# Differential heads stored unscaled with their norm applied once per row tile, and index query stacks filled from SBUF to SBUF, in a hybrid attention layer

## The chip, the cores and the metric

The kernel runs on one core of one Trainium2 chip. The metric is the device time in microseconds (us) of one execution; several executions are timed and their median is given. The core has five engines that matter here: TensorE (PE: matmuls and transposes), VectorE (DVE), ScalarE (ACT), GpSimd (POOL) and SyncE (SP, which issues nearly all transfers). Each engine takes its instructions from a queue of its own, strictly in order; an instruction that waits holds up all that stand behind it on the same engine.

## The reference

One transformer layer for 1024 rows of width 1024. An input projection feeds three token mixers whose outputs are concatenated (256 + 512 + 256 columns), projected, added to the input and normalised; a SwiGLU feed-forward block with a second norm follows. Two of the mixers matter here.

```python
# differential attention: 4 heads, two softmaxes each
logits = einsum('bthmd,bshmd->bhmts', qblk, k) * scale - slope * dist      # masked by chunk
p = softmax(logits)
attn = p[:, :, 0] - lam * p[:, :, 1]
o = einsum('bhts,bshe->bthe', attn, v)                                     # 128 columns per head
o = rms_norm(o, subln_g) * (1.0 - lam_init)     # o * rsqrt(mean(o*o) + 1e-5) * g, per row and head

# sparse attention: an indexer with 8 heads of width 32 picks 256 keys per row
idx_logits = einsum('bthd,bsd->bths', qi, ki)
score = einsum('bth,bths->bts', wi * idx_scale, relu(idx_logits))          # masked by chunk
_, sel = top_k(score, 256)
```

## The kernel before, in words

Rows are cut into 8 tiles of 128. Float32 products are made exact enough by splitting each operand into a rounded part and a rest (names ending in h and l) and running three matmuls per product: `mm3` (L179 to L182) issues all three. An engine's instruction order is not written out: the kernel is traced in program order, a list scheduler with a cost model orders each engine's queue, and memory and buffers are given out by the same framework, which makes an instruction wait where it reuses memory that something else still reads. Program order and `high_priority` blocks set the priorities.

The stages, by the time at which they run in the profiled execution:

- To 48 us: x is loaded, transposed and split; `proj_ik` and `proj_iq` (L240 to L252) project the index key `kst` and the index queries. `hq[c]`, `lq[c]` (c = 0, 1) hold the rounded and rest parts of four query heads each, 32 partitions per head.
- From 48 to 143 us: the index scores. Each of the 8 heads needs a stack `qst` of 128 partitions: rounded, rest, rounded, rest of its 32 rows. Before the change `hq[c]` and `lq[c]` are stored into a DRAM tile `qd[c]` (L294, L295) and four stacks are read back, each by one transfer whose source pattern has a leading dimension of 2 with step 0 (L298 to L300). `index` (L358 to L375) makes 48 steps (8 heads by 6 row tiles): matmuls `psi` (L365), a relu on ScalarE into `rl` (L367), and a weighted sum into the score buffer `sc_all` on VectorE (L370, L372).
- In between run steps of the generator `fill`, which makes the remaining projections in the order of `FILL_ORDER`: first the values of heads 0 and 1 ("v0", four steps of 48 matmuls `psn` each, L325 to L335), then the queries and keys of head 0 ("b0", four half projections of 24 matmuls `psp`). `INDEX_FILLS` says after how many index steps how many fill steps are traced; L713 to L717 do that and then run `FIRST_FILL` more steps.
- From 143 to 431 us: the differential heads, 32 units of a head and a row tile (`diff_unit`, L637 to L659), in the order of `UNITS`, with further fill steps and steps of a bisection for the 256th score (`bisect`, on VectorE and ScalarE) between them as `FILLS`, `STEPS_A` and `STEPS_D` say. A unit runs two softmaxes without normalising (`softmax`, L600 to L614: the sums of the exponentials are s1 and s2), forms p1 - lam * (s1/s2) * p2 (L645 to L648), transposes it on PE and multiplies it with the values into the one PSUM buffer of its kind, `pso` (`attend`). Then ScalarE squares `pso` scaled by 1/s1 and sums it (L655), `rsqrt` forms the norm factor with one VectorE and one POOL instruction (L192 to L198), VectorE multiplies it by 1/s1 (L657) and writes the scaled and weighted tile `ob` (L658), which SyncE stores into the DRAM tile `mixd[i]` (L659).
- From 431 to about 690 us: the sparse heads (`dsa_pair`), and per row tile `mix_in` (L801 to L812), which loads `mixd[t]` as `mx`, transposes it and splits it for the output projection (`out_half`); then the first norm (`finish1`).
- To 1372 us: the feed-forward block and the second norm.

Of the kernel before, what the change touches and what calls it, by code (L numbers as in the profile page):

```python
# [9 lines left out]
F32 = mybir.dt.float32  # L10
# [4 lines left out]
AF = mybir.ActivationFunctionType  # L15
OP = mybir.AluOpType
AX = mybir.AxisListType

P = 128
S = 1024  # L20
DM = 1024
NT = S // P
# [8 lines left out]
NH = 4  # L31
SLOPES = [2.0 ** (-2.0 * (h + 1)) for h in range(NH)]
# [3 lines left out]
EPS = 1e-5  # L36
# [4 lines left out]
LASTN = 6  # L41
FILL_ORDER = ["v0", "b0", "b1", "b2", "v2", "b3", "vc", "c0", "g", "c1"]
INDEX_FILLS = [(11, 1), (6, 1), (13, 1), (8, 1), (2, 1), (8, 1)]
FIRST_FILL = 1
GMLP_ORDER = ["uv", "u", "u", "u", "v", "v", "vs", "vs", "s", "s"]
UNITS = [
# [39 lines left out]
def pieces(n):  # L86
    r = []
    o = 0
    while o < n:
        w = min(512, n - o)  # L90
        if 0 < n - o - w < 256:
            w = n - o - 256
        r.append((o, max(w, 256)))
        o += w
    return r
# [3 lines left out]
def trunk(  # L99
# [5 lines left out]
    nc = tc.nc  # L105
# [6 lines left out]
    pool = ctx.enter_context(tc.tile_pool(name="pool", bufs=1))  # L112
    psum = ctx.enter_context(tc.tile_pool(name="psum", bufs=2, space=bass.MemoryType.PSUM))
    dram = ctx.enter_context(tc.tile_pool(name="dram", bufs=1, space=bass.MemoryType.DRAM))
# [9 lines left out]
    def st(name, shape=(P, 1024), dt=F32R):  # L124
        return tl("st", 12, name, shape, dt)
# [10 lines left out]
    def small(name, w=1, dt=F32, bufs=5):  # L136
        return pool.tile([P, w], dt, tag=f"s_{name}", bufs=bufs, name=name)
# [7 lines left out]
    def ps_qk(name):  # L145
        return psum.tile([P, 512], F32, tag="qk", bufs=3, name=name)

    def ps_av(name):
        return psum.tile([P, 512], F32, tag="av", bufs=1, name=name)

    def f(ap):
        return ap.bitcast(F32)

    V, A, GP = nc.vector, nc.scalar, nc.gpsimd
# [5 lines left out]
    def rawload(src, name, shape):  # L160
        raw = tl("raw", 2, f"raw_{name}", shape)
        nc.sync.dma_start(raw, src)
        return raw

    def wsplit(raw, name, shape, lo_eng, hi=None, lo=None):
        if hi is None:
            hi = tl("hi", 3, f"hi_{name}", shape, F32R)
            lo = tl("lo", 3, f"lo_{name}", shape, F32R)
        if lo_eng is GP:
            GP.tensor_scalar(hi, raw, 1.0, 1.0, op0=OP.mult, op1=OP.mult)  # L170
        else:
            A.activation(hi, raw, AF.Copy)
        sub(lo_eng, lo, raw, f(hi))
        return hi, lo

    def wload(src, name, shape, lo_eng, hi=None, lo=None):
        return wsplit(rawload(src, name, shape), name, shape, lo_eng, hi, lo)

    def mm3(ps, lh, ll, rh, rl, first, last):  # L179
        nc.tensor.matmul(ps, lh, rh, start=first, stop=False)  # L180
        nc.tensor.matmul(ps, lh, rl, start=False, stop=False)  # L181
        nc.tensor.matmul(ps, ll, rh, start=False, stop=last)  # L182

    def row_bcast(vec, n):
        return bass.AP(tensor=vec.tensor, offset=vec.offset, ap=[[0, P], [1, n]])
# [3 lines left out]
    mhalf = pool.tile([P, 8], F32, name="mhalf")  # L189
    V.memset(mhalf, -0.5)  # L190

    def rsqrt(o, var, eps, w, pre=None):  # L192
        t = small(f"rv{w}", w)
        if pre is None:
            V.tensor_scalar(t, var, eps, None, op0=OP.add)  # L195
        else:
            V.tensor_scalar(t, var, pre, eps, op0=OP.mult, op1=OP.add)
        GP.tensor_tensor(o, t, mhalf[:, 0:w], OP.pow)  # L198
# [48 lines left out]
    def proj_iq(c, half):  # L247
        w0, w = ((256, 256), (0, 512))[half]
        ps = proj_t(*iqw[c], P, half, w0, w)
        o = half * 512 + w0 - 256  # L250
        A.activation(hq[c][:, o:o + w], ps[:, w0:w0 + w], AF.Copy)
        sub(V, lq[c][:, o:o + w], ps[:, w0:w0 + w], f(hq[c][:, o:o + w]))  # L252

    iqw, hq, lq = [], [], []

    def load_iq(c):
        if c == 1:
            riq.append(rawload(win[:, :, I_Q + P:I_Q + 2 * P], "iq1", [P, KC, P]))
        iqw.append(wsplit(riq[c], f"iq{c}", [P, KC, P], V))
        hq.append(st(f"hq{c}", (P, 768)))  # L260
        lq.append(st(f"lq{c}", (P, 768)))
# [23 lines left out]
    V.tensor_copy(iw, pw[:, 0:64].rearrange("p (a b) -> p a b", a=NT))  # L285

    qst = []
    qd = [dram.tile([4, 2, 32, 768], F32, name=f"qd{c}") for c in range(2)]
    for c in range(2):
        if c == 1:  # L290
            load_iq(1)
            proj_iq(1, 0)
            proj_iq(1, 1)
        nc.sync.dma_start(qd[c][:, 0], f(hq[c]))  # L294
        nc.sync.dma_start(qd[c][:, 1], f(lq[c]))  # L295
        for j in range(4):
            q = st(f"qst{c}_{j}", (P, 768))
            rep = qd[c][j].rearrange("r p c -> (r p) c")  # L298
            rep = bass.AP(tensor=rep.tensor, offset=rep.offset, ap=[[0, 2], [768, 64], [1, 768]])
            nc.sync.dma_start(f(q), rep)  # L300
            qst.append(q)

    lamv = []
    for nm, (a, b) in enumerate(((lq1, lk1), (lq2, lk2))):
# [5 lines left out]
        r = small(f"lr{nm}", 1, bufs=1)  # L310
# [3 lines left out]
    neglam = small("neglam", 1, bufs=1)  # L314
# [3 lines left out]
    subg = pool.tile([P, P], F32, name="subg")  # L318
# [34 lines left out]
    o = 0  # L353
# [121 lines left out]
    junk, junk_a = junk2[:, 0], junk2[:, 1]  # L475
# [118 lines left out]
    def prob_tiles(i, c):  # L594
        if c * (i + 1) <= KC:
            t = pp("pt")
            return [t[:, j * P * (i + 1):(j + 1) * P * (i + 1)] for j in range(c)]
        return [pp("pt") for _ in range(c)]

    def softmax(i, m, q, kh, kl, bias, slope, p):  # L600
        n = P * (i + 1)
        nm = None
        sm = small("sm")
        for o, w in pieces(n):
            ps = ps_qk("psq")
            nc.tensor.matmul(ps[:, 0:w], q[:, i * P:(i + 1) * P], kh[:, o:o + w], start=True, stop=False)
            nc.tensor.matmul(ps[:, 0:w], q[:, i * P:(i + 1) * P], kl[:, o:o + w], start=False, stop=True)
            w = min(w, n - o)
            prev = BIG if nm is None else nm
            nm = small(f"nm{o}")  # L610
            V.tensor_tensor_reduce(out=p[:, o:o + w], in0=ps[:, 0:w], in1=bias[:, o:o + w], scale=-slope, scalar=prev,  # L611
                                   op0=OP.add, op1=OP.min, accum_out=nm)
        A.activation(p[:, 0:n], p[:, 0:n], AF.Exp, bias=nm, scale=-1.0, accum_out=sm)  # L613
        return p, sm  # L614
# [10 lines left out]
    def attend(i, a, vsl, ps):  # L625
        nk = i + 1
        for j0 in range(0, nk, 4):
# [6 lines left out]
            for j in range(jn):  # L634
                nc.tensor.matmul(ps, at[:, j * P:(j + 1) * P], vsl(j0 + j), start=(j0 + j == 0), stop=(j0 + j == nk - 1))  # L635

    def diff_unit(h, i, qs, kh, kl, vb):  # L637
        n = P * (i + 1)
        bias = dist[:, S - n:S]
        p1, p2 = prob_tiles(i, 2)  # L640
        _, s1 = softmax(i, 0, qs[0], kh[0], kl[0], bias, SLOPES[h], p1)
        _, s2 = softmax(i, 1, qs[1], kh[1], kl[1], bias, SLOPES[h], p2)
        r1, r2 = small("r1"), small("r2")
        sn = small("sn", 1, bufs=3)
        GP.tensor_tensor(sn, s1, neglam, OP.mult)  # L645
        V.reciprocal(r2, s2)
        V.tensor_tensor(r2, r2, sn, OP.mult)
        V.scalar_tensor_tensor(p1[:, 0:n], p2[:, 0:n], r2, p1[:, 0:n], op0=OP.mult, op1=OP.add)  # L648
        V.reciprocal(r1, s1)
        ps = ps_av("pso")  # L650
        attend(i, p1, lambda j: vb[:, j], ps[:, 0:P])
        ss = small("ss")
        ob = tl("o", 4, "ob", (P, P))
        rs = small("rs")
        A.activation(junk_a[:, 0:P], ps[:, 0:P], AF.Square, scale=r1, accum_out=ss)  # L655
        rsqrt(rs, ss, EPS, 1, pre=1.0 / P)
        V.tensor_tensor(rs, rs, r1, OP.mult)  # L657
        V.scalar_tensor_tensor(ob, ps[:, 0:P], rs, subg, op0=OP.mult, op1=OP.mult)  # L658
        nc.sync.dma_start(mixd[i][:, 256 + h * P:256 + (h + 1) * P], ob)  # L659

    bits = {e: list(range(31, -1, -1)) for e in "ad"}

# [6 lines left out]
    def run(gen, n=100):  # L669
        for _ in range(n):  # L670
            if next(gen, 0) == 0:
                break
# [22 lines left out]
    ix = index(range(8))  # L695
# [11 lines left out]
    fill = stream([g_ for k_ in FILL_ORDER for g_ in units[k_]])  # L707

    def ensure(qk, v, u):
        while min(made.get(qk + "q", 0), made.get(qk + "k", 0)) < 1 + u // 4 or made.get(v, 0) < 1 + u // 2:  # L710
            next(fill)

    for q, r_ in INDEX_FILLS:  # L713
        run(ix, q)
        run(fill, r_)
    run(ix)
    run(fill, FIRST_FILL)  # L717
    nstep = {"a": STEPS_A, "d": STEPS_D}

    def scale_rows(o, r, e):  # L720
# [80 lines left out]
    def mix_in(t):  # L801
        mx = tl("raw", 2, "mx")
        nc.sync.dma_start(mx, mixd[t])
        nh, nl, shp = f"mTh{t}", f"mTl{t}", (P, KC, P)
        if t in (3, 4):
            ms[t] = pp(nh, shp, F32R), pp(nl, shp, F32R)
        else:
            ms[t] = tl("hi", 3, nh, shp, F32R), tl("lo", 3, nl, shp, F32R)
        transpose_split(mx, *ms[t], 0, n=6)
        v = mx[:, 6 * P:].rearrange("p (a b) -> p a b", a=2)  # L810
        A.activation(ms[t][0][:, 6:8], v, AF.Copy)
        sub(GP, ms[t][1][:, 6:8], v, f(ms[t][0][:, 6:8]))  # L812
# [240 lines left out]
    for hh in range(2):  # L1053
# [8 lines left out]
        for t in range(4):  # L1062
# [4 lines left out]
            for d in range(2):  # L1067
                ps = acc[2 * t + d]
# [38 lines left out]
```

## Time and profile before

| | |
|---|---|
| median of 3 runs | 1370.33 us (1369.95 to 1374.3) |
| the profiled execution's own time | 1374.44 us |
| its span from first to last instruction | 1372.5 us |
| mean granted TensorE clock | 0.968 of full |
| transfers | 107685 packets, 127.46 MB |

The profile records one execution. It gives for every engine the busy time and its share of the span, in windows of time the busy time of each engine beside the granted TensorE clock (1.00 is full speed) and the transfers, for every group of instructions (line, engine, operation, output <- input, shape) its count, its busy time, the mean time of one in ns and the idle time of its engine just ahead of it, and for waits who waited for whom: total us, how often, the longest. "PEld" is the loading of weights into the PE array, which overlaps matmuls. A name such as L658 is a line of the kernel before.

### The profile page before, as it was taken

Reading aid. Unit: us, or ns where it says so; the run is one execution under the profiler, and the core shown is the slowest. Engines: PE = TensorE matmul, PEld = TensorE weight load, DVE = VectorE, ACT = ScalarE, POOL = GpSimd, SP = SyncE. Lnnn points to the kernel's source line nnn. Section 1 sums busy time; section 2 is a strip of 40 time slices with the busy share of each in tenths; the row PEclk is TensorE's granted clock in tenths of the full one; section 3 lists DMA queues with packets and bytes.
Section 4 is the critical chain, followed back from the end, with each engine's and each line's share of the span. In section 5 each row is a group of like instructions: output and inputs, shape, how many; then the busy total and the mean of one; then the engine's idle time right before and its main releaser. Section 6 shows DMA issues by size and latency. Waiting matters only on the chain.

```text
span 1372.5 us, 17547 instructions
## 1 busy us (share of the span) xinstructions
PE 1265.1 (92%) x6444; PEld 1052.3 (77%) x6444; DVE 909.6 (66%) x1797; ACT 554.2 (40%) x1033; POOL 328.5 (24%) x262
## 2 busy tenths in 40 slices
PE   7559888879998989899999999999999999999997
PEld 6457676777887977567888888888888888888886
DVE  5138999997767885737498676666776674357325
ACT  4136576766975443632134223222232232214220
POOL 0202332122141273202044332333223300000003
PEclk9879999899999999899999999999999999999999
DMA  6222111101113102244222223232222259418401
GB/s 198 74 75 66 51 30 49 36 26 45 30 43 83 40 26 86 61 150 173 69 90 77 80 74 92 77 93 81 73 92 77 77 203 364 153 63 326 148 0 62
DMA packets 107685, 127.46 MB, mean 93 GB/s; under 512 B 8144, under 2 KB 80720, under 8 KB 107600
## 3 DMA queue, kind: packets, MB, share of 16 engines
q1 hardware_dynamic: 106448, 122.15, 27.4%
q10 hardware_dynamic: 1152, 4.19, 1.0%
q8 instruction: 51, 0.84, 0.3%
q14 instruction: 34, 0.28, 0.1%
HBM read 97.49 MB, written 25.69 MB: 90 GB/s over the span
## 4 chain that ended last, share of the span: by engine, by line
PE 51%; DVE 1%; issue 1%; DMA 0%; POOL 0%; ACT 0%; DVEq 0%; SPq 0%; POOLq 0%; ACTq 0%
PE p L182 9%; PE p L181 9%; PE p L180 9%; PE psd L180 6%; PE psd L181 6%; PE psd L182 6%; PE psz L180 1%; PE psz L182 1%; PE psz L181 1%; PE pu L182 0%; PE pu L180 0%; PE pu L181 0%; PE pg L182 0%; PE pg L180 0%; PE pg L181 0%
## 5 line engine op out<-in xcount | busy, mean ns | idle before, releaser
L501 ACT ACTIVATE junk<-sc_all,cf_a 128x768 bf16<-128x768 f32 (+2 forms) x93 | 96.4, 1037 | 26.6 <-DVE cf_a L493 16.3
L180 PE MATMUL psn<-hi_n,xTh 128*128 128x256 f32 x320 | 94.6, 296 | 0.0
L181 PE MATMUL psn<-lo_n,xTh 128*128 128x256 f32 x320 | 94.4, 295 | 0.0
L182 PE MATMUL psn<-hi_n,xTl 128*128 128x256 f32 x320 | 94.0, 294 | 0.0
L198 POOL TENSOR_TENSOR lrs<-rv,mhalf 128x1 f32<-128x1 f32 x16 | 20.6, 1286 | 306.5 <-DVE rv L195 306.5
L613 ACT ACTIVATE pt<-pt,nm 128x128 f32<-128x128 f32 (+7 forms) x96 | 73.7, 769 | 41.3 <-DVE nm L611 38.2
L970 POOL TENSOR_TENSOR s<-raw_u 128x512 f32<-128x512 f32 x20 | 29.3, 1466 | 242.7 <-DMA raw_u<-in_w_gu_dram 202.9
L496 DVE TENSOR_SCALAR_CACHE_REDUCE junk<-sc_all,cf_d 128x384 bf16<-128x384 f32 (+2 forms) x93 | 69.1, 743 | 1.8
L180 PEld LDWEIGHTS psn<-hi_n,xTh 128*128 128x128 f32 x320 | 64.2, 201 | 1.6 <-issue 0.5
L181 PEld LDWEIGHTS psn<-lo_n,xTh 128*128 128x128 f32 x320 | 64.1, 200 | 1.0 <-issue 0.2
L182 PEld LDWEIGHTS psn<-hi_n,xTl 128*128 128x128 f32 x320 | 63.9, 200 | 0.7 <-issue 0.3
L180 PE MATMUL p<-x1Th,gh 128*128 128x512 f32 x160 | 62.2, 389 | 0.0
L181 PE MATMUL p<-x1Tl,gh 128*128 128x512 f32 x160 | 62.2, 389 | 0.0
L182 PE MATMUL p<-x1Th,gl 128*128 128x512 f32 x160 | 62.2, 389 | 0.0
L996 DVE TENSOR_TENSOR th<-p,tp 128x512 f32<-128x512 f32 x20 | 13.8, 692 | 72.5 <-DMA hd<-th 60.2
L365 PE MATMUL psi<-kst,qst 128*128 128x512 f32 (+1 forms) x80 | 27.8, 386 | 33.4 <-DMA qst<-qd 21.9
L372 DVE SCALAR_TENSOR_TENSOR sc_all<-rl,iw,sc_all 128x384 f32<-128x384 f32 (+5 forms) x42 | 39.3, 995 | 26.8 <-ACT rl L367 26.5
L1012 ACT ACTIVATE sg<-tp 128x512 f32<-128x512 f32 x20 | 12.6, 631 | 103.7 <-DVE tp L1011 103.7
L993 ACT ACTIVATE tp<-p 128x512 f32<-128x512 f32 x20 | 12.0, 599 | 95.3 <-DVE th L1018 82.4
L635 PE MATMUL pso<-vb,ats 128*128 128x128 f32 x288 | 40.6, 288 | 10.0 <-DVE ob L658 3.7
L635 PEld LDWEIGHTS pso<-vb,ats 128*128 128x128 f32 x288 | 38.5, 202 | 13.6 <-DVE ob L658 4.6
L631 PE MATMUL psa<-ident,pt 128*128 128x128 f32 x144 | 26.2, 300 | 23.9 <-DVE pt L648 13.2
(666 smaller groups left out, 4082.5 us busy)
## 6 DMA issues: line engine op xcount, KB each, us to landing
raw_g<-in_w_gu_dram SPq DMA_DIRECT2D x22, 512.0 KB
raw_u<-in_w_gu_dram SPq DMA_DIRECT2D x22, 512.0 KB
hd<-th SPq DMA_DIRECT2D x22, 512.0 KB
raw_n<-in_w_in_dram SPq DMA_DIRECT2D x10, 512.0 KB
x<-in_x_dram SPq DMA_DIRECT2D x8, 512.0 KB
raw_wo<-in_w_out_dram SPq DMA_DIRECT2D x8, 512.0 KB
mx<-mixd SPq DMA_DIRECT2D x8, 512.0 KB
y<-x1d SPq DMA_DIRECT2D x8, 512.0 KB
```

Source lines behind the costliest of these rows:

```text
L180: nc.tensor.matmul(ps, lh, rh, start=first, stop=False)
L181: nc.tensor.matmul(ps, lh, rl, start=False, stop=False)
L182: nc.tensor.matmul(ps, ll, rh, start=False, stop=last)
L198: GP.tensor_tensor(o, t, mhalf[:, 0:w], OP.pow)
L365: nc.tensor.matmul(ps[:, 0:w], qst[h][:, (i - 2) * P:(i - 1) * P], kst[:, o:o + w], start=True, stop=True)
L372: V.scalar_tensor_tensor(SC[i], r[:, 0:n], wcol, SC[i], op0=OP.mult, op1=OP.add)
L496: V.tensor_scalar(junk[:, 0:P * (i + 1)], SC[i], f(cf)[:, j:j + 1], None, op0=OP.is_ge, op1=OP.add, accum_out=cnt[:, j:j + 1])
L501: A.activation(junk_a[:, 0:P * (i + 1)], SC[i], AF.Sign, bias=f(cf)[:, j:j + 1], accum_out=cnt[:, j:j + 1])
L613: A.activation(p[:, 0:n], p[:, 0:n], AF.Exp, bias=nm, scale=-1.0, accum_out=sm)
L631: nc.tensor.transpose(pt[:, j * P:(j + 1) * P], a[:, (j0 + j) * P:(j0 + j + 1) * P], ident)
L635: nc.tensor.matmul(ps, at[:, j * P:(j + 1) * P], vsl(j0 + j), start=(j0 + j == 0), stop=(j0 + j == nk - 1))
L970: GP.tensor_tensor(a[:, 0:4], u[:, 0:4], u[:, 4:8], OP.add)
```

## The change

In the differential heads, `diff_unit` no longer forms 1/s1. s1 and the sum of squares of the unscaled `pso` are written into two tables for all row tiles and heads, `s1_all` and `ss_all`; the factor of p2 is formed by one VectorE instruction in the place of one on POOL and one on VectorE; `pso` is copied unscaled into `ob` by ScalarE. The new `rms_rows`, called in `mix_in` when a row tile is loaded, forms the factors (ss/128 + 1e-5 * s1 * s1) ** -0.5 for its four heads at once and multiplies the 512 columns by them and by the weights `subg`.

In the index, the DRAM tiles `qd` go: each stack is filled by four transfers of 32 partitions by 768 columns straight from `hq[c]` and `lq[c]`, 32 transfers in all. Two fill steps are traced ahead of the index steps and none behind them, so that 8 fill steps in place of 7 precede the units. Each block of index steps is traced under `issue_after(tail[0])`: its matmuls are ordered on PE behind the last matmul that `mm3` issued so far. No wait across engines is added by that.

```diff
-FIRST_FILL = 1
+FIRST_FILL = 2
...
+    tail = [None]
+
     def mm3(ps, lh, ll, rh, rl, first, last):
         nc.tensor.matmul(ps, lh, rh, start=first, stop=False)
         nc.tensor.matmul(ps, lh, rl, start=False, stop=False)
-        nc.tensor.matmul(ps, ll, rh, start=False, stop=last)
+        tail[0] = nc.tensor.matmul(ps, ll, rh, start=False, stop=last).ins
...
-    qd = [dram.tile([4, 2, 32, 768], F32, name=f"qd{c}") for c in range(2)]
...
-        nc.sync.dma_start(qd[c][:, 0], f(hq[c]))
-        nc.sync.dma_start(qd[c][:, 1], f(lq[c]))
         for j in range(4):
             q = st(f"qst{c}_{j}", (P, 768))
-            rep = qd[c][j].rearrange("r p c -> (r p) c")
-            rep = bass.AP(tensor=rep.tensor, offset=rep.offset, ap=[[0, 2], [768, 64], [1, 768]])
-            nc.sync.dma_start(f(q), rep)
+            for b in range(4):
+                nc.sync.dma_start(f(q[32 * b:32 * b + 32]), f((hq, lq)[b % 2][c][32 * j:32 * j + 32]))
             qst.append(q)
...
-    def softmax(i, m, q, kh, kl, bias, slope, p):
+    def softmax(i, m, q, kh, kl, bias, slope, p, sm=None):
...
-        sm = small("sm")
+        if sm is None:
+            sm = small("sm")
...
+    s1_all = pool.tile([P, NT, NH], F32, name="s1_all")
+    ss_all = pool.tile([P, NT, NH], F32, name="ss_all")
+
     def diff_unit(h, i, qs, kh, kl, vb):
...
-        _, s1 = softmax(i, 0, qs[0], kh[0], kl[0], bias, SLOPES[h], p1)
+        _, s1 = softmax(i, 0, qs[0], kh[0], kl[0], bias, SLOPES[h], p1, s1_all[:, i, h:h + 1])
         _, s2 = softmax(i, 1, qs[1], kh[1], kl[1], bias, SLOPES[h], p2)
-        r1, r2 = small("r1"), small("r2")
-        sn = small("sn", 1, bufs=3)
-        GP.tensor_tensor(sn, s1, neglam, OP.mult)
+        r2 = small("r2")
         V.reciprocal(r2, s2)
-        V.tensor_tensor(r2, r2, sn, OP.mult)
+        V.scalar_tensor_tensor(r2, s1, neglam, r2, op0=OP.mult, op1=OP.mult)
         V.scalar_tensor_tensor(p1[:, 0:n], p2[:, 0:n], r2, p1[:, 0:n], op0=OP.mult, op1=OP.add)
-        V.reciprocal(r1, s1)
         ps = ps_av("pso")
         attend(i, p1, lambda j: vb[:, j], ps[:, 0:P])
-        ss = small("ss")
         ob = tl("o", 4, "ob", (P, P))
-        rs = small("rs")
-        A.activation(junk_a[:, 0:P], ps[:, 0:P], AF.Square, scale=r1, accum_out=ss)
-        rsqrt(rs, ss, EPS, 1, pre=1.0 / P)
-        V.tensor_tensor(rs, rs, r1, OP.mult)
-        V.scalar_tensor_tensor(ob, ps[:, 0:P], rs, subg, op0=OP.mult, op1=OP.mult)
+        A.activation(junk_a[:, 0:P], ps[:, 0:P], AF.Square, accum_out=ss_all[:, i, h:h + 1])
+        A.activation(ob, ps[:, 0:P], AF.Copy)
         nc.sync.dma_start(mixd[i][:, 256 + h * P:256 + (h + 1) * P], ob)
+
+    def rms_rows(i, mx):
+        t, rs = small("rmt", NH, bufs=2), small("rmr", NH, bufs=2)
+        V.scalar_tensor_tensor(t, s1_all[:, i], EPS, s1_all[:, i], op0=OP.mult, op1=OP.mult)
+        V.scalar_tensor_tensor(t, ss_all[:, i], 1.0 / P, t, op0=OP.mult, op1=OP.add)
+        GP.tensor_tensor(rs, t, mhalf[:, 0:NH], OP.pow)
+        o = mx[:, 256:768].rearrange("p (h c) -> p h c", h=NH)
+        V.tensor_tensor(o, o, rs[:, :, None].to_broadcast([P, NH, P]), OP.mult)
+        V.tensor_tensor(o, o, subg[:, None, :].to_broadcast([P, NH, P]), OP.mult)
...
+    run(fill, FIRST_FILL)
     for q, r_ in INDEX_FILLS:
-        run(ix, q)
+        with tc.issue_after(tail[0]):
+            run(ix, q)
         run(fill, r_)
     run(ix)
-    run(fill, FIRST_FILL)
...
     def mix_in(t):
         mx = tl("raw", 2, "mx")
         nc.sync.dma_start(mx, mixd[t])
+        rms_rows(t, mx)
```

## The prediction

> **What bounds the kernel now.** I read the page first. TensorE is the busiest engine, and nothing else comes near its share.
>
> ```profile
> PE 1265.1 (92%) x6444; PEld 1052.3 (77%) x6444; DVE 909.6 (66%) x1797; ACT 554.2 (40%) x1033; POOL 328.5 (24%) x262
> ```
>
> So 1372.5 - 1265.1 = 107 us of the span have no matmul running, and the question is where those gaps lie and which of them the change touches. The busy time by windows answers that (each column: us busy and, in brackets, instructions, then granted clock, DMA share, GB/s).
>
> ```profile
> 48.00:63.00 15.00, 0.08 (x2) 0.07 (x1) 0.69 (x1) 0.60 (x1) 3.28 (x2) 0.65 0.15 57
> 63.00:142.60 79.60, 61.09 (x344) 54.74 (x345) 46.55 (x59) 39.79 (x92) 15.03 (x8) 0.87 0.19 65
> ```
>
> ```profile
> 142.60:320.00 177.40, 147.52 (x824) 126.21 (x823) 167.90 (x626) 122.76 (x288) 44.80 (x60) 0.93 0.15 40
> 320.00:431.00 111.00, 99.00 (x601) 86.90 (x600) 75.33 (x235) 84.41 (x190) 29.49 (x38) 0.95 0.17 44
> ```
>
> From 48 to 142.6 (index scores and first projections) TensorE is idle for 14.9 + 18.5 = 33.4 us, and the clock granted is below full. From 142.6 to 431 (differential heads) it is idle for 29.9 + 12.0 = 41.9 us; up to 320 VectorE is busy 95% of the time, so VectorE leads there. Two stages hold 75 of the 107 us, and the change edits both. PE's waits between 48 and 143 name the first one's cause:
>
> ```profile
> PE psi L365 <- DMA qst<-qd: 21.9, 5, 14.9
> PE psi L365 <- ACT vb L343: 9.8, 1, 9.8
> PE psi L365 <- ACT rl L367: 1.7, 1, 1.7
> ```
>
> ```profile
> ACT vb L343 <- DMA qd<-hq: 13.2, 1, 13.2
> ```
>
> All 33.4 us stand ahead of psi, the index matmul. 21.9 wait for the query stacks coming back from DRAM; the 9.8 wait for ScalarE, whose blocked instruction waits itself for the store of hq to DRAM. The projection matmuls that could fill the gap are queued behind psi on PE's in-order queue.
>
> **Part 1: stacks from SBUF to SBUF, two projection steps first.** SyncE's timeline shows the old way, and one SBUF-to-SBUF copy that the kernel already makes:
>
> ```profile
> 40.38 0.56 SPq L295 DMA_DIRECT2D qd<-lq  x1
> ...
> 52.37 14.73 SPq L300 DMA_DIRECT2D qst<-qd  x4
> ```
>
> ```profile
> 190.69 0.47 SPq L591 DMA_DIRECT2D b1k_h<-b1k_h  x1
> ```
>
> The read-back can't be issued before the store has landed, at 52.37. Then it moves slowly; the windows of the first read-back and of the b1k_h copy:
>
> ```profile
> 54.00:66.00 12.00, 3.04 (x12) 2.98 (x13) 1.03 (x3) 1.79 (x4) 0.00 (x0) 0.50 0.12 48
> ```
>
> ```profile
> 191.60:192.70 1.10, 0.71 (x4) 0.24 (x2) 1.10 (x9) 0.00 (x0) 0.05 (x1) 1.00 0.52 119
> ```
>
> The read-back uses 0.12 of 16 engines (two) at 48 GB/s. The 128-KB copy is issued at 190.69 and done by 192.7, 2.0 us later. The new copies are 32 of 96 KB, and I price each issue like b1k_h, 0.47 us: the first four stacks are issued from 40.4 to 47.9, the other four within 7.5 us of hq1 and lq1, which are ready near 49.4 (two evictions behind 48.0), so all have landed by about 59. That is the bound from below; above, the four old issues average 14.73/4 = 3.7 us. I take 0.47 because it is the same kind of transfer on a free queue. Behind these issues on SyncE stand the loads of b1's weights, projected only after b0's.
>
> Next, what TensorE does instead. Its timeline gives the prices:
>
> ```profile
> 47.65 0.39 PE L182 MATMUL psp<-xTh,lo_iq 128*128 128x512 f32 x1
> ...
> 73.85 0.28 PE L180 MATMUL psn<-hi_n,xTh 128*128 128x256 f32 x1
> ...
> 75.89 0.28 PE L182 MATMUL psn<-hi_n,xTl 128*128 128x256 f32 x1
> ...
> 137.31 0.39 PE L180 MATMUL psp<-xTh,hi_b0k 128*128 128x512 f32 x1
> ...
> 142.53 0.39 PE L182 MATMUL psp<-xTh,lo_b0k 128*128 128x512 f32 x1
> ```
>
> Eighteen psn matmuls start from 73.85 to 75.89, 0.12 apart: a value step of 48 takes 5.8 us. Twenty-four psp matmuls start from 137.31 to 142.53, 0.227 apart: a half projection takes 5.45. The index matmuls:
>
> ```profile
> L365 PE MATMUL psi<-kst,qst x80: 274/393/796, 63.0 to 135.0; 128*128 128x512 f32 x40, 128*128 128x384 f32 x24, 128*128 128x256 f32 x16
> ```
>
> 40 x 0.23 + 24 x 0.17 + 16 x 0.12 = 15.2 us. So from 48.0 to 142.9 TensorE does 4 x 5.8 + 15.2 + 3 x 5.45 = 54.8 us of work in 94.9; 33.4 are waits and 6.7 the slow clock. The most that can go is 40.
>
> What the new order leaves: two value steps run first, 48.0 to 59.6, and hide the copies; if that cover were gone, the wait would be the copies' few us. Then come the 48 index steps in six blocks, each held behind the fill before it, with VectorE adding up scores:
>
> ```profile
> L372 DVE SCALAR_TENSOR_TENSOR sc_all<-rl,iw,sc_all 128x384 f32<-128x384 f32 (+5 forms) x42 | 39.3, 995 | 26.8 <-ACT rl L367 26.5
> ...
> L370 DVE TENSOR_SCALAR sc_all<-rl,iw 128x384 f32<-128x384 f32 (+5 forms) x6 | 3.5, 588 | 17.0 <-ACT rl L367 16.9
> ```
>
> 42.8/48 = 0.9 us of VectorE and 15.2/48 = 0.32 of TensorE per step. Taking for each block the longer of VectorE's steps and TensorE's steps plus its fill: 11 steps 9.9, 6 steps 7.7, 13 steps 11.7, 8 steps 8.0, 2 steps 6.1, 8 steps 8.0: 51.4 us, so it ends at 111. The wait that the block order adds sits ahead of psi on PE; behind it is only later fill, which doesn't need it. The end to compare it with, on VectorE:
>
> ```profile
> 140.42 0.23 DVE L374 MEMSET sc_all<- 64x64 f32 x2
> ```
>
> Scores are complete 140.6 - 111 = 29.6 us earlier; the projections (now with b0k's second half, 142.9 + 5.45) 37 earlier. I take 33, bounds 12 (below, rival 3) and 40.
>
> **Part 2: differential heads unscaled.** Of each of the 32 units VectorE loses four instructions; the product with sn takes over a POOL step at equal VectorE count:
>
> ```profile
> L658 DVE SCALAR_TENSOR_TENSOR ob<-pso,rs,subg 128x128 f32<-128x128 f32 x32 | 11.5, 358 | 0.4
> L657 DVE TENSOR_TENSOR rs<-rs,r 128x1 f32<-128x1 f32 x32 | 11.2, 349 | 10.1 <-POOL rs L198 9.5
> ...
> L649 DVE RECIPROCAL r<-sm 128x1 f32<-128x1 f32 x32 | 4.9, 154 | 1.1 <-ACT pt L613 1.0
> L197 DVE TENSOR_SCALAR rv<-ss 128x1 f32<-128x1 f32 x32 | 4.7, 148 | 6.2 <-ACT junk L655 6.1
> ```
>
> That is 32.3 us busy and 17.8 of idle time ahead of them. ScalarE gains a copy like this one, 32 x 0.275 = 8.8 us, with 81 us idle (288.4 - 207.2) to hide it:
>
> ```profile
> L728 ACT ACTIVATE oc<-psc 128x128 f32<-128x128 f32 x16 | 4.4, 275 | 24.8 <-PE psc L755 24.5 <-issue 0.3
> ```
>
> How much reaches the end? PE's waits from 142.6 to 320, and the one row from 320 to 431 that the change removes outright:
>
> ```profile
> PE psa L631 <- DVE pt L648: 11.7, 10, 2.4
> ...
> PE pso L635 <- DVE ob L658: 3.7, 2, 2.7
> ```
>
> ```profile
> PE psa L631 <- DVE rs L657: 2.7, 1, 2.7
> ```
>
> Certain are 3.7 + 2.7 = 6.4 us, waits for instructions that are gone. At most it is 41.9, all of PE's idle time in the stage. Between them: about half the units finish before 320, where VectorE leads, so some 16 us busy and 9 idle leave its queue there, but PE has only 29.9 idle and both engines can't be full at once. I take 18, near half of 41.9; next late is PE itself.
>
> **Part 3: the norm per row tile.** Each of 8 tiles gets two small products, one power on POOL and two passes over 128x512 ahead of its transposes. Nearest rows: a broadcast product of that size, the same size at its slowest, and POOL's power at width 8.
>
> ```profile
> L422 DVE TENSOR_TENSOR g<-g,gmu 128x512 f32<-128x512 f32 x4 | 2.8, 689 | 0.1
> ```
>
> ```profile
> L1014 DVE TENSOR_TENSOR th<-th,tp 128x512 f32<-128x512 f32 x20 | 30.4, 1518 | 0.7
> ...
> L198 POOL TENSOR_TENSOR grs<-rv,mhalf 128x8 f32<-128x8 f32 x4 | 7.0, 1744 | 25.8 <-DVE rv L197 24.3 <-DVE sm L740 1.4
> ```
>
> 1.4 us of passes plus 0.3 on VectorE per tile, 3.3 at worst. POOL's power lies beside other work of VectorE and only lengthens the chain. The tightest place for the rest is this one:
>
> ```profile
> 640.00:660.00 20.00, 19.86 (x105) 16.20 (x104) 19.34 (x31) 7.32 (x13) 5.67 (x5) 1.00 0.52 180
> 660.00:690.00 30.00, 30.00 (x137) 24.68 (x136) 12.40 (x21) 2.29 (x4) 1.89 (x2) 1.00 0.11 39
> ```
>
> Three tiles there add 5.1 us (10 at worst) to a VectorE with 0.7 free, though it recovers after 660. I take 3, bounds 0 and 10; a gain has no source, since nothing is removed there.
>
> **Sum.** -33 - 18 + 3 = -48 on the profiled execution: 1374.44 - 48 = 1326.4. That execution is 4.1 us above the median of the runs, 1370.33, so the prediction is 1322. Everything behind 690 runs on PE without gaps and shifts whole.
>
> A rule speaks against part 1. The Trainium skill, page "DMA: Bandwidth & Descriptors", section "Anatomy of one DMA", puts about 2.0 us of fixed cost on each transfer, and the section "Rules for kernel authors" advises one large transfer over many small. By it 32 copies one after another, at an estimated 2.2 us each, are done 70 us after 40.4, scores end near 116 and the sum is 5 us less, 1327. The b1k_h copy's 2.0 us from issue to landing agrees with the figure; its 0.47 us of issue says that copies overlap.
>
> **The rivals.**
>
> 1. Only part 1 gains. VectorE's freed time turns into waits for exp, bisection counts or PE. For it: PE is 89% busy after 320. Against it: VectorE's 95% before 320. -33 + 3 = -30: 1340.
> 2. PE never waits again in either stage: -40 - 42 = -82: 1288. Against it: one av buffer and tile-by-tile softmax remain.
> 3. The hold does not do what it says: fills don't slip between the index matmuls but stand behind them. Then 48.0 + 11.6 + 43.2 + 11.6 + 21.8 = 136 against 148.4 for the same work: -12, in all -27: 1343. Against it: psn and psi interleave in the timeline now.
> 4. Copies paid one after another at 2.0 us each, as the rule has it: scores end at 40.4 + 64 + 5.4 = 110, the same as VectorE's pace, at 2.2 a few us later: 1327.
> 5. Slower: each 96-KB copy lands on one engine, at half of the 48 GB/s that two gave: 24 GB/s, 4.1 us, 131 us for all. The last stack lands at 171, its six steps of 0.9 end the scores at 177, 36 later than now; -18 + 3 leaves +21: 1391. It decides the sign from 40.4 + 32c + 5.4 = 140.6 + 15, c = 3.4 us a copy. Against it: the b1k_h copy ran at 0.52 of 16 engines. The skill's DMA page, section "Why a DMA increments its semaphore by 16 and not by 1", lets the slowest dimension set the engines: 32 rows would get 16, and the old leading 2 the two that the trace shows.
>
> **How the numbers follow.** Chances: forecast 0.54, rival 1 0.16, rival 2 0.07, rival 3 0.11, rival 4 0.06, rival 5 0.04, and 0.02 that gains and costs cancel. The forecast's own range, from the halves of its bounds, is 1306 to 1338. Taking in rivals 1, 3 and 4 gives 1302 to 1350; rivals 2 and 5 stay out. Faster by over 0.3% (about what a measurement of this kernel can tell from none): 0.94; within: 0.02; slower: 0.04.
>
> **What would show it.** Right: no psi wait for a DMA over 2 us; psn matmuls from 48 to 59; scores complete near 111; clock at full from 48 on; VectorE under 85% in the heads stage, which is some 50 us earlier at its end; PE still 95% busy around the row tiles. Wrong: psi waiting for its stacks or for fills (part 1), PE idle in the heads stage unchanged with VectorE idle too (part 2), or transposes of mx waiting for VectorE several us a tile (part 3).

## The result and the profile after

The kernel after takes 1338.57 us (median of four runs, 1336.68 to 1340.02) against 1370.14 for the kernel before on the same chip: a ratio of 0.9764, 95% interval 0.9739 to 0.979, so 31.6 us are gone. The forecast had 48, and 1322: the time lies 16.6 us above it, just outside the forecast's own range of 1306 to 1338 and inside the wider one of 1302 to 1350. The profiled execution took 1339.51 us, its span 1337.7.

The first rows of the page of after, and its waits of PE from 20 to 130 us (us in total, times, longest):

```profile
PE 1254.7 (94%) x6444; PEld 1046.0 (78%) x6444; DVE 902.2 (67%) x1701; ACT 556.3 (42%) x1065; POOL 315.2 (24%) x206
```

```profile
PE psp L182 <- DVE b0q L569: 3.1, 1, 3.1
PE psa L630 <- DVE pt L648: 1.6, 1, 1.6
...
PE psi L363 <- DVE b0q L569: 1.0, 1, 1.0
```

Of the 33.4 us that psi waited, for its stacks and for ScalarE, 1.0 is left, and no wait for a stack, as forecast. But VectorE, which was to lose 32.3 us in the heads and gain 13 or so in the row tiles, went from 909.6 only to 902.2. The stages, in the windows of after (scores complete at 121.4, last head stored at 391.9, last C unit at 583.6):

```profile
48.00:121.40 73.40, 67.68 (x399) 59.70 (x398) 56.90 (x77) 46.02 (x114) 22.32 (x14) 0.98 0.31 79
121.40:270.00 148.60, 119.73 (x691) 103.19 (x690) 142.49 (x483) 107.37 (x259) 21.77 (x15) 0.92 0.13 35
270.00:391.90 121.90, 111.94 (x689) 98.05 (x689) 86.17 (x243) 96.21 (x231) 28.09 (x19) 0.98 0.18 47
```

VectorE still leads up to 270: 142.49 of 148.6 is 96%. TensorE's idle time between complete scores and the last head, 41.9 us before, is still 28.9 + 10.0 = 38.8. The four milestones of after, on VectorE, ScalarE and PE (xcount, then ns shortest/median/longest, first and last start):

```profile
L372 DVE MEMSET sc_all<- x6: 112/112/112, 111.3 to 121.4; 64x64 f32 x6
L653 ACT ACTIVATE ob<-pso x32: 254/270/288, 116.7 to 391.9; 128x128 f32<-128x128 f32 x32
L733 ACT ACTIVATE oc<-psc x16: 260/278/279, 407.3 to 583.6; 128x128 f32<-128x128 f32 x16
L182 PE MATMUL pg<-x1Th,gh x16: 389/389/395, 664.0 to 692.7; 128*128 128x512 f32 x16
```

The same four in the kernel before:

```profile
L374 DVE MEMSET sc_all<- x6: 112/112/112, 135.4 to 140.5; 64x64 f32 x6
L658 DVE SCALAR_TENSOR_TENSOR ob<-pso,rs,subg x32: 331/350/740, 160.5 to 430.4; 128x128 f32<-128x128 f32 x32
L728 ACT ACTIVATE oc<-psc x16: 258/277/280, 446.3 to 617.3; 128x128 f32<-128x128 f32 x16
L180 PE MATMUL pg<-x1Th,gh x16: 387/389/390, 698.6 to 727.7; 128*128 128x512 f32 x16
```

The last starts of the first three and the first of the fourth come 19.1, 38.5, 33.7 and 34.6 us earlier. So scores were complete 10 us later than forecast, the heads ended 38.5 us earlier and not some 50, and about 4 us were given back behind them.

### The profile page after: what moved, and what is told of

It reads as the page before. It is cut to its first block, busy times and chain, and to the rows that moved or that the text cites. A ratio compares the mean times of both kernels' runs of the same rounds, so it can differ in the third digit from the quotient of the medians.

```text
span 1337.7 us, 17441 instructions
## 1 busy us (share of the span) xinstructions
PE 1254.7 (94%) x6444; PEld 1046.0 (78%) x6444; DVE 902.2 (67%) x1701; ACT 556.3 (42%) x1065; POOL 315.2 (24%) x206
## 4 chain that ended last, share of the span: by engine, by line
PE 64%; DVE 6%; ACT 4%; issue 2%; POOL 2%; DMA 1%; DVEq 0%; SPq 0%; ACTq 0%; POOLq 0%
PE p L183 9%; PE p L184 9%; PE p L182 9%; PE psd L182 6%; PE psd L184 6%; PE psd L183 6%; PE psz L182 2%; PE psz L184 2%; PE psz L183 2%; ACT junk L499 2%; PE psc L760 2%; PE psa L754 1%; ACT pt L612 1%; DVE pt L610 1%; PE pst L210 1%
## 5 line engine op out<-in xcount | busy, mean ns | idle before, releaser
L612 ACT ACTIVATE pt<-pt,nm 128x768 f32<-128x768 f32 (+7 forms) x96 | 73.8, 770 | 45.5 <-DVE nm L610 40.4
L976 POOL TENSOR_TENSOR s<-raw_u 128x512 f32<-128x512 f32 x20 | 32.1, 1606 | 213.6 <-DVE s12l L158 146.0
L1018 ACT ACTIVATE sg<-tp 128x512 f32<-128x512 f32 x20 | 12.6, 631 | 128.2 <-DVE tp L1017 128.2
L610 DVE CUSTOM_DVE_ANT_0 pt<-psq,dist 128x512 f32<-128x512 f32 (+3 forms) x72 | 38.6, 542 | 14.3 <-PE psq L606 13.1
L630 PEld LDWEIGHTS psa<-ident,pt 128*128 128x128 f32 x144 | 17.1, 149 | 37.3 <-DVE pt L648 24.7
L370 DVE SCALAR_TENSOR_TENSOR sc_all<-rl,iw,sc_all 128x384 f32<-128x384 f32 (+5 forms) x42 | 42.9, 1079 | 3.7 <-ACT rl L365 3.6
L158 POOL TENSOR_TENSOR s<-s,raw_g 128x512 f32<-128x512 f32 x20 | 43.6, 2181 | 0.0
```

The costliest lines, as they stand in the source:

```text
L158: eng.tensor_tensor(o, a, b, OP.subtract)
L370: V.scalar_tensor_tensor(SC[i], r[:, 0:n], wcol, SC[i], op0=OP.mult, op1=OP.add)
L630: nc.tensor.transpose(pt[:, j * P:(j + 1) * P], a[:, (j0 + j) * P:(j0 + j + 1) * P], ident)
L976: GP.tensor_tensor(a[:, 0:4], u[:, 0:4], u[:, 4:8], OP.add)
```

## The experiments

Each kernel was timed beside the kernel before on the same chip, in three groups; ratios are to the kernel before, with 95% intervals. The medians of the kernel before were 1371.42, 1371.14 and 1375.34 us in the three groups (1370.14 where the kernel after was timed), so that across groups a few us are not told apart. The theory at the start (A) was that the terms add up as forecast and only part 2 was too large; the rival (B) that the parts pay for each other.

**One part alone.** part1 is the kernel after with the old `diff_unit` and without `rms_rows`; part23 is the old index stage and order with the new heads. copies and order split part 1:

```
copies:  FIRST_FILL = 1, run(fill, FIRST_FILL) behind run(ix), no issue_after;
         qst filled from hq/lq; old diff_unit
order:   FIRST_FILL = 2 ahead of the index steps, issue_after;
         qst through qd as before; old diff_unit
```

> Part 1 alone: stacks filled from SBUF to SBUF, two value steps ahead of the index steps and the hold; the heads keep their old norm and there are no row-tile passes. Theory A (the terms add up as forecast, only part 2 was mis-sized): part 1 is worth 33 us or a little more, 1334 to 1338, and nearly the whole gain of the change is here. Theory B (part 1 gives VectorE's work of the heads an earlier start but not a shorter one, and part 2 pays for what the stage would lose): part 1 alone gives only 18 to 25 us, 1345 to 1352, and VectorE is over 95% busy up to the last head.

> Parts 2 and 3 alone: heads stored unscaled and the norm per row tile; query stacks through DRAM and the old order of the index steps. By the forecast's terms -18 + 3 = -15 us, 1355. Theory A: -1 to -5 us, 1365 to 1369, since VectorE stays the leader before 320 and waits for ScalarE's counts after it. Theory B: about -8 to -12 us, 1358 to 1362, and the two parts do not add up with part1.

> The copies from SBUF to SBUF alone, index steps ahead of all projection steps as before, one value step behind them. If the wait for the stacks is the cost, this has most of part 1: PE waits for psi fall from 33 us to under 10, and the time is 25 to 30 us below before, 1340 to 1345. If the order is what counts (PE fills the 11 us under the copies), it has at most half, 1353 or more.

> The order alone: two value steps first and the hold, stacks still through DRAM. The two steps cover 48 to 59.6, the stacks of the second half still come late: psi waits for DMA fall from 21.9 us to some 10, and the time is 10 to 17 us below before, 1353 to 1360. If the order alone hides the round trip, it comes within 5 us of part1 and the copies were not needed.

Measured: part1 1347.17 us, ratio 0.9824 (0.9776 to 0.9871); part23 1377.99, 1.005 (1.003 to 1.0071); copies 1339.88, 0.9771 (0.9732 to 0.9811); order 1386.52, 1.0102 (1.0057 to 1.0147).

The copies alone have the whole gain of the change, 31.5 us. Both other parts make the kernel slower by themselves: the order by 15 us, the heads and row tiles by 6.6. So part23 lies outside what both theories gave it. part1's 24.2 us lie in B's range, though not its sign: VectorE is busy 84% from complete scores to the last head there (242.3 of 287.2 us), not over 95%. Beside the order part 2 is worth something, alone it isn't. The order alone missed its own forecast of 1353 to 1360 by 26 us. The profile of copies, its scores on VectorE and its largest waits of PE from 48 to 150:

```profile
L368 DVE TENSOR_SCALAR sc_all<-rl,iw x6: 420/642/2450, 49.5 to 53.9; 128x384 f32<-128x384 f32 x1, 128x512 f32<-128x512 f32 x1, 128x640 f32<-128x640 f32 x1, 128x768 f32<-128x768 f32 x1
L370 DVE SCALAR_TENSOR_TENSOR sc_all<-rl,iw,sc_all x42: 606/944/3094, 54.6 to 109.5; 128x384 f32<-128x384 f32 x7, 128x512 f32<-128x512 f32 x7, 128x640 f32<-128x640 f32 x7, 128x768 f32<-128x768 f32 x7
L372 DVE MEMSET sc_all<- x6: 112/112/112, 103.7 to 110.8; 64x64 f32 x6
```

```profile
PE psq L605 <- DVE b0k_l L158: 3.7, 1, 3.7
PE psa L629 <- DVE pt L646: 2.6, 2, 1.4
PE psn L182 <- DVE lq L158: 2.1, 1, 2.1
```

No wait for psi is left, without any projection ahead of it: the stacks need no cover. Scores are complete at 110.8. VectorE starts on them at 49.5, with the six products of the first head; in after it starts at 60.3, with the two value steps in front, and ends as much later:

```profile
L368 DVE TENSOR_SCALAR sc_all<-rl,iw x6: 421/586/755, 60.3 to 64.0; 128x384 f32<-128x384 f32 x1, 128x512 f32<-128x512 f32 x1, 128x640 f32<-128x640 f32 x1, 128x768 f32<-128x768 f32 x1
L370 DVE SCALAR_TENSOR_TENSOR sc_all<-rl,iw,sc_all x42: 605/1010/2895, 64.7 to 119.7; 128x384 f32<-128x384 f32 x7, 128x512 f32<-128x512 f32 x7, 128x640 f32<-128x640 f32 x7, 128x768 f32<-128x768 f32 x7
```

The forecast had put the end of the scores in after at 111; that copies ends there is luck. The forecast had the score steps start at 59.6 and take 51.4 us; in both kernels they take 61. In copies VectorE waits for 13 of them, mostly for ScalarE; in after the score work took 46.8 us where the forecast had 42.8, and 9.6 us went to other VectorE work between the score steps, for b0 and the first units, which the forecast's sum left out.

In order, the stacks still go through DRAM. The waits of PE and of ScalarE there, from 48 to about 150, show what the value steps are put in front of:

```profile
PE psi L367 <- ACT rl L369: 26.3, 2, 23.2
```

```profile
ACT rl L369 <- DMA qd<-hq: 29.1, 1, 29.1
```

SyncE's timeline shows the second store of hq issued only when the first read-back has been:

```profile
51.90 14.20 SPq L302 DMA_DIRECT2D qst<-qd  x4
66.20 7.31 SPq L296 DMA_DIRECT2D qd<-hq  x1
```

ScalarE, on which the index stands, waits for that store in both orders (13.2 us before, 29.1 here). psi still waits 30.2 us in all, near the 33.4 of before, but now behind the value steps: scores are complete 16 us later than before, at 156.6, and the last head is stored 12 us later.

**Which part of the way through DRAM.** The kernel before, with each read-back split in two:

```
-            rep = bass.AP(..., ap=[[0, 2], [768, 64], [1, 768]])
-            nc.sync.dma_start(f(q), rep)
+            for b in range(2):
+                nc.sync.dma_start(f(q[64 * b:64 * b + 64]), rep)   # rep: 64 rows
```

> The kernel before, each stack read back from DRAM by two transfers of 64 partitions in place of one whose leading dimension is 2. If two engines for the read-back are the cost, the reads land within 3 us each, the psi waits for DMA fall from 21.9 us to under 6, the one of 9.8 behind the second store goes too, and the time is 18 to 28 us below before, 1343 to 1352. If the round trip through DRAM is the cost, it gains under 10 us, 1361 or more.

Measured: 1350.31 us, ratio 0.9825 (0.9778 to 0.9872), 25 us below before (18 to 31 by the interval), as the first of the two expectations had it. The window of its first read-back, the landings, and the one wait of psi that is left:

```profile
52.00:57.00 5.00, 0.87 (x2) 0.82 (x3) 0.00 (x0) 0.12 (x1) 0.00 (x0) 0.56 0.73 184
```

```profile
DMA to landing us min/median/max: 3.0/3.9/9.6
```

```profile
PE psi L365 <- DMA qst<-qd: 8.4, 1, 8.4
```

The same bytes move at 184 GB/s and a DMA share of 0.73, where the old pattern had 48 and 0.12. The reads land in 3.9 us in the median and not within 3, and psi keeps 8.4 us of wait and not under 6. So some 25 of the 31.5 us were the two-engine read-back. The trip through DRAM itself would be the other 6 or so; that is not shown, since the intervals of dram64's and copies' ratios overlap.

**Do parts add up?** copies23 is copies with parts 2 and 3; copies2 and norows are copies23 and after without `rms_rows`, so that their heads stay without the norm; fill_last is after with `run(fill, FIRST_FILL)` moved behind `run(ix)`, the hold kept.

> Copies from SBUF to SBUF and parts 2 and 3, index steps first as before (no hold, one value step behind them). Theory C: VectorE leads from the first score step to 320, so the two value steps ahead cost what they keep it waiting, 10 us (first score product at 64.6 with them, at 54.6 without). Then this is 6 to 10 us faster than the kernel after, 1329 to 1333. Rival D: parts 2 and 3 give nothing unless PE has its projections in hand (alone on before they cost 7 us); then this is no faster than copies alone, 1340 to 1347.

> As copies23, but the rows of mx are not multiplied by the norm factors and the weights: the heads' columns reach the projection unscaled, and rms_rows is left out. Theory C with part 3 at its forecast size: 3 us below copies23. Theory E: the passes of the row tiles hold VectorE while it leads the stage of the C units too, and cost 8 us; then 1321 to 1325 and the time from the last head to the last mx transpose is as in copies, 221 us, not 230.

> The kernel after without rms_rows: the heads' columns reach the projection unscaled. Forecast: 3 us faster, 1335. Theory E: 7 to 9 us faster, 1330, since from the last head (391) to the last mx transpose (621) the kernel after takes 9 us longer than part1 does. If it is the same as after, the 9 us are the C units' own waits.

> The kernel after with its two value steps behind the index steps; the hold stays. Theory C: VectorE starts its score products at 55 in place of 64.7, and the time falls by 6 to 10 us, 1329 to 1333. If the hold, and not the fills ahead, is what makes the order cost, it stays at 1338 or more, and PE waits for psi come back.

Measured: copies23 1344.54, 0.98 (0.9769 to 0.9832); copies2 1341.78, 0.9783 (0.9758 to 0.9808); norows 1333.96, 0.9731 (0.9703 to 0.9759); fill_last 1338.42, 0.976 (0.9741 to 0.9779).

Part 3 costs 4.6 us in after's order (1338.57 - 1333.96) and 2.8 in copies' (1344.54 - 1341.78); the intervals of the ratios overlap in both pairs, so that neither is clear of noise, but both agree with the 3 forecast better than with the 8 of theory E. Part 2 without part 3 gains 13.2 us in the new order (1347.17 - 1333.96, intervals apart) and nothing in the old one (1341.78 - 1339.88 is +1.9). Theory C falls: copies23 and fill_last are both above its 1329 to 1333. In fill_last VectorE starts its scores at 49.6 and completes them 14 us sooner than in after, and its last head is stored 3 us later:

```profile
L372 DVE MEMSET sc_all<- x6: 112/112/112, 100.0 to 107.2; 64x64 f32 x6
```

```profile
L653 ACT ACTIVATE ob<-pso x32: 254/268/287, 123.5 to 395.1; 128x128 f32<-128x128 f32 x32
```

The time is the same as after's. fill_last falls in the range of theory C's rival, that the hold is the cost, but without its sign: no wait for psi comes back. copies23 falls in rival D's range; whether D is right stays open, since no run has fill_last's order without parts 2 and 3. What the order decides shows in PE's waits between 121 and 700 for the two VectorE results that stand at the end of a unit; part1 first, then copies, after, and copies23:

```profile
PE psa L629 <- DVE pt L646: 21.8, 15, 5.8
PE pso L633 <- DVE ob L656: 9.0, 6, 5.7
...
PE psq L604 <- DVE ob L656: 3.6, 2, 2.3
```

```profile
PE psa L629 <- DVE pt L646: 13.1, 12, 2.4
...
PE pso L633 <- DVE ob L656: 4.6, 3, 2.8
...
PE psq L604 <- DVE ob L656: 0.7, 1, 0.7
```

```profile
PE psa L630 <- DVE pt L648: 23.5, 12, 4.5
```

```profile
PE psa L630 <- DVE pt L648: 25.3, 15, 4.3
```

In the new order PE waited 9.0 + 3.6 = 12.6 us for ob; part 2 takes ob off VectorE and gains 13. In the old order it waited 5.3 us for ob, which go too, but the wait for pt rises from 13.1 to 25.3. That these waits make up the whole difference is argued and not shown. Some of the gain is lost behind the heads: the last head comes 17.3 us sooner in norows than in part1 (409.5 to 392.2) and 5.9 sooner in copies2 than in copies (400.8 to 394.9), while the feed-forward block starts 13.3 sooner and 2.1 later. Why PE waits more for pt in one order and not in the other was not tried.

**How much of VectorE's time reaches the end.**

```
halfbits:  -    bits = {e: list(range(31, -1, -1)) for e in "ad"}
           +    bits = {"a": list(range(31, -1, -1)), "d": list(range(31, 15, -1))}
ob_vector: -        A.activation(ob, ps[:, 0:P], AF.Copy)
           +        V.tensor_copy(ob, ps[:, 0:P])
```

> The kernel after with 16 of the 32 rounds of VectorE's bisection left out (the thresholds of its three blocks stay coarse). VectorE loses 16 x 2.9 = 47 us of work between the scores and the last head. Theory F (freed VectorE time turns into waits for PE, exp and counts): the last head comes under 10 us earlier, 1329 or more. Theory G (VectorE's work is the bound of the stage and part 2 only freed too little of it): 25 us or more earlier, 1313 or less.

> The kernel after with the copy of ob on VectorE in place of ScalarE: VectorE gets back some 32 x 0.25 = 8 us, ScalarE loses 8.8. Theory F: within 3 us of after, 1336 to 1342. Theory G: 5 to 8 us slower, 1344 to 1347.

Measured: halfbits 1321.99, 0.9621 (0.9596 to 0.9647); ob_vector 1343.09, 0.9773 (0.9741 to 0.9806). The page of halfbits, and its window from 121.4, where the scores of after are complete, to its last head, beside the window of after:

```profile
PE 1249.8 (95%) x6444; PEld 1044.3 (79%) x6444; DVE 866.0 (66%) x1557; ACT 555.8 (42%) x1065; POOL 316.5 (24%) x206
```

```profile
121.40:377.90 256.50, 228.78 (x1387) 199.63 (x1388) 190.38 (x582) 204.74 (x492) 52.26 (x34) 0.97 0.17 45
```

```profile
121.40:391.90 270.50, 231.67 (x1378) 201.23 (x1377) 228.66 (x725) 203.58 (x489) 49.86 (x33) 0.95 0.15 41
```

228.66 - 190.38 = 38.3 us less on VectorE, not the 47 expected, shorten the stage by 14.0: 0.37 us per us freed. Over the whole kernel 902.2 - 866.0 = 36.2 us bring 1338.57 - 1321.99 = 16.6, or 0.46; the two were timed in different groups, and by the ratios it is 19.6 us, or 0.54. The result lies between theory F and theory G: the time freed here is worth about half or less. In halfbits PE is busy 89% of the window and VectorE 74%, so neither leads all through; what is left is waiting for one another within a unit. ob_vector's median lies between the two ranges, and by its ratio it cannot be told from after; its trace shows where the cost would come from, PE waiting for ob again:

```profile
PE pso L634 <- DVE ob L653: 9.3, 6, 3.5
```

**A version without the row passes on VectorE.**

The edit, shortened:

```
fold (rms_rows): -  V.tensor_tensor(o, o, rs[:, :, None].to_broadcast(...), OP.mult)
                 -  V.tensor_tensor(o, o, subg[:, None, :].to_broadcast(...), OP.mult)
                 +  for h in range(NH): A.activation(o_h, o_h, AF.Copy, scale=rs[:, h:h + 1])
fold (mix_in):   +  A.activation(oh, v, AF.Copy, scale=subg)      # subg: one per partition
                 +  V.scalar_tensor_tensor(ol, v, subg, oh, op0=OP.mult, op1=OP.subtract)
```

> The kernel after with part 3 taken off VectorE: the norm factors are applied by four ScalarE scalings of 128x128 per row tile, and the weights of the norm in the evictions behind the transposes of mx, where they cost no instruction. Without any row passes the kernel after is 4.6 us faster; this should keep 3 to 5 of them, 1333.5 to 1336. If ScalarE's 1.1 us a tile sits in the chain as VectorE's 1.4 did, it gains nothing, 1338 to 1340.

Measured: 1335.38 us, ratio 0.9718 (0.9692 to 0.9745), 3.2 us below after's median in another group; as the first expectation had it, but the intervals of the two ratios just overlap. By its median it is the fastest kernel here that computes the whole reference. After the transposes the weight of the norm is one value per partition, so it rides on an eviction that is there anyway.

## Why the prediction was off by 16 us

The sign and the wide range came as forecast; the terms did not. On medians, part 1 alone -24.2 (forecast -33), part 2 on top of it -13.2 (-18), part 3 +4.6 (+3): together -32.8, and -31.6 measured. All three errors point the same way. Rival 1's 1340 is closer to the time than the forecast, but by luck: its 33 us from part 1 and nothing from part 2 did not come either. And the copies alone are as fast as the whole change.

- "Two value steps run first, 48.0 to 59.6, and hide the copies" failed as a gain, and part 1 is the largest error, 9 us. The copies needed no hiding: copies alone gives 31.5 us, nearly the 33 that part 1 was forecast at, and part1, which adds the steps and the hold, only 24.2. The text had itself priced the missing cover at "the copies' few us". The intervals of the two ratios overlap, but the four runs of each, in one group, do not (1338.97 to 1341.82 against 1345.51 to 1349.04). That the order costs beside stacks through DRAM is shown by order, 15 us above before. Inside the order, the sum of 51.4 us for the score steps was too short by 10, as said above.
- "I price each issue like b1k_h, 0.47 us" was low. SyncE's first and last copies in after:

```profile
39.16 2.54 SPq L298 DMA_DIRECT2D qst<-hq  x4
41.79 0.54 SPq L298 DMA_DIRECT2D qst<-lq  x1
...
66.71 3.92 SPq L298 DMA_DIRECT2D qst<-lq  x6
```

  The 32 issues took 0.59 us in the median (0.51 to 1.82), and the last is issued at 70, not by 57, with weight loads in between. It cost nothing: psi never waits for a copy. Rivals 4 and 5 are out, by the landings in copies:

```profile
DMA to landing us min/median/max: 2.0/2.2/4.0
```

  The Trainium skill, page "DMA: Bandwidth & Descriptors", section "Anatomy of one DMA", puts a fixed cost of about 2.0 us on a transfer issued by GpSimd. SyncE issues these; none landed sooner than 2.0 us after its issue, and issued 0.6 us apart they overlap. What the same page of the Trainium skill, section "Why a DMA increments its semaphore by 16 and not by 1", says of the slowest dimension and the engines agrees with the DMA shares, 0.12 before and 0.73 in dram64.
- "That is 32.3 us busy" was the wrong size. Between part1 and norows, which differ by part 2 alone, VectorE's total falls from 904.7 to 889.0, by 15.7. Part of the durations that were summed were not work but hold (last section): rs of one column took 349 ns in the mean, a reciprocal of the same shape 154, and those 32 x 0.195 = 6.2 us can fall on a later instruction when rs goes. More of it is that neighbouring VectorE instructions overlap in the profile: in part1 all their durations add up to 998.9 us where the busy time is 904.7, and of the 27.4 us of ob, rs and rv only 17.4 have no other VectorE instruction beside them.
- "I take 18, near half of 41.9" took the rate too high and the order as given. The rate measured by halfbits is 0.4 to 0.5 per us freed; 15.7 us at that rate are 6 to 8. Part 2 gave 13 in one order and nothing in the other. The 41.9 us of idle time were not the base either: with part 1 alone TensorE idles 49.0 us in that stage (287.2 - 238.2), and with part 2 too 38.8. What became of part of the freed time is rival 1's mechanism: in after VectorE waits 18.8 us for ScalarE's counts ahead of fl_a between 48 and 392, in part1 8.6 between 48 and 408:

```profile
L500 DVE TENSOR_TENSOR fl_a<-cnt_a,lim 128x3 int32<-128x3 f32 x31 | 10.7, 344 | 18.8 <-ACT junk L499 18.7
```

```profile
L500 DVE TENSOR_TENSOR fl_a<-cnt_a,lim 128x3 int32<-128x3 f32 x31 | 6.3, 205 | 8.6 <-ACT junk L499 8.5
```

- "Three tiles there add 5.1 us (10 at worst) to a VectorE with 0.7 free" and "I take 3": right in size, 2.8 to 4.6, neither clear of noise.
- Of the signs named: psi without DMA waits, psn from 47.5 to 59, the clock at 1.00 from 48 to 100 (0.92 from there to 121) and TensorE without gaps around the row tiles (30.0 of the 30 us from 610 to 640) came true; scores near 111 and 50 us at the heads' end did not. VectorE under 85% in the heads stage came out, 84.5%, but told nothing: it was 84.3% before.

What stays open: why the same units cost 7 us more or less when their projections are traced in another order. Theory C, VectorE's late start, was the one reason tried, and it fell.

## What to carry to other kernels

When a transfer is slow, look first at the share of DMA engines it uses: here an access pattern, not the memory, was some 25 of 31.5 us. A cover is worth something only for a wait that is left once the transfer is mended; ask what the engine behind it (here VectorE) does meanwhile. In a stage where two engines hand work to each other, do not value the time taken off one at one for one: here 38 us of bisection less shortened the stage by 14, and part 2's 16 us were worth 13 in one order and nothing in the other. So test parts in each other's presence.

## What the runs showed of the hardware

VectorE instructions with two inputs in SBUF stood still here while GpSimd ran a split, a subtraction of 128x1024 with two inputs. In after, GpSimd's splits and the VectorE instructions beside them (start, us):

```profile
117.16 2.37 POOL L158 TENSOR_TENSOR lo_b2q<-raw_b2q,hi_b2q 128x1024 fp32r<-128x1024 f32 x1
```

```profile
117.12 2.69 DVE L648 SCALAR_TENSOR_TENSOR pt<-pt,r 128x256 f32<-128x256 f32 x1
```

```profile
262.97 2.34 POOL L158 TENSOR_TENSOR lo_b3k<-raw_b3k,hi_b3k 128x1024 fp32r<-128x1024 f32 x1 [1.86 <-issue]
```

```profile
256.58 0.21 DVE L647 SCALAR_TENSOR_TENSOR r<-s_all,neglam,r 128x1 f32<-128x1 f32 x1
...
263.28 2.05 DVE L647 SCALAR_TENSOR_TENSOR r<-s_all,neglam,r 128x1 f32<-128x1 f32 x1
```

A product of one column, 0.21 us otherwise, took 2.05 and ended with GpSimd's subtraction, at 265.3. A count with one tensor input ran beside another split at its usual pace:

```profile
165.67 2.37 POOL L158 TENSOR_TENSOR lo_n<-raw_n,hi_n 128x1024 fp32r<-128x1024 f32 x1
```

```profile
162.80 0.87 DVE L494 TENSOR_SCALAR_CACHE_REDUCE junk<-sc_all,cf_d 128x640 bf16<-128x640 f32 x1
...
165.85 0.88 DVE L494 TENSOR_SCALAR_CACHE_REDUCE junk<-sc_all,cf_d 128x640 bf16<-128x640 f32 x1
```

The Trainium skill, page "GPSIMD Engine Reference", section "Key points", says that GpSimd shares its SBUF interfaces with VectorE and contends with VectorE instructions that have two SBUF inputs; these rows agree, and show that the wait can last the whole GpSimd instruction. Beside GpSimd's power on four columns (rmr, 1.3 us) no such hold is seen: the 128x512 product of mx and rmr took 0.71 us there and 0.68 in the median. All this is read from the traces alone: no run took the splits off GpSimd.
